# More pairs of an up projection by seven block products, with a worked-out order for the stage

## The chip, the cores and the metric

The kernel runs on one core of a Trainium2 chip. The metric is the device time of one execution in microseconds; the median of three timed runs is given, and one more execution was taken with the hardware profiler.

## What is computed

One transformer block over 512 tokens of width 1024, in fp32. Attention comes first; the change lies in the feed-forward part behind it:

```python
h = rmsnorm(x, mlp_pre_g[i])
gu = h @ w_gate_up[i].astype(h.dtype)          # 1024 -> 2 x 2816
a, u = jnp.split(gu, [D_FF], axis=-1)
a = causal_dwconv(a, conv_w[i], conv_b[i])     # 3 taps along the tokens
y = (jax.nn.gelu(a, approximate=True) * u) @ w_down[i].astype(h.dtype)
x = x + rmsnorm(y, mlp_post_g[i])
```

## The kernel before

Everything is kept transposed: features on the 128 partitions, the 512 tokens along the free axis. Each fp32 operand is split into a high part (ACT rounds it to the float32r type) and a low part (DVE subtracts), and each product is three matmuls: high by high, low by high, high by low (`mm3`).

The hidden width, 2816, makes 22 tiles of 128 rows of `a` and as many of `u`; tile j of both is called pair j here. Pairs 0 to 6 use the input before its normalization (`h2`; the factor `r3` is applied to the results, by POOL too), later ones the normalized input `hn`. A plain pair is two tiles of 8 chunks of 3 matmuls of 512 columns. For the pairs in `BLOCKED`, a 2 x 2 block scheme over (chunk parity) by (token half) needs seven block products in place of eight, each of 4 chunks of 3 matmuls of 256 columns. Its operands are sums: those of the input (`ht`, from `half_sums`) are made once, those of the weights per pair. `gs` holds a pair's four weight blocks. `block_sums_ahead` loads two of them to `y` and two to `x`; POOL then issues three accumulating DMAs, which make y a pair of sums and x two further ones out of y. `blocked_weights` loads the first two blocks once more, for the products that need them plain, and splits all four into high and low parts; each of the six `wh` buffers takes one part of 1024 columns. `blocked_tile` collects the seven products in four PSUM banks and puts them together with one ACT copy and five DVE operations. Then come the convolution (one ACT instruction, two DVE taps), the gelu on ACT, the product with `u` on DVE (mul), and the split of y (`keep_y`: yhi on ACT, ylo on DVE).

The order on each engine is set by a scheduler at compile time, by dependencies and priorities; `keep_in_program_order` pins an instruction behind the one traced before it on its engine. Most of this stage isn't pinned, so the scheduler mixes work of neighbouring pairs and of the down stage that follows. That stage begins with one plain row of tiles (c = 6), in whose shadow DVE makes sums of the stage's results (`sums_of`, from the y's) and the low parts of its weights, then goes on with a plain group of weights and further seven-product groups. PSUM has eight banks, under the tags s (3), mm (2), t (2), o (1). Large SBUF buffers come by tags too: `u` (26), `p` (6), `wr` (2, raw weights), `wh` (6), `kn`, `pt`, `tt`.

Of the kernel before, what the change touches and what calls it, by code (L numbers as in the profile page):

```python
# [81 lines left out]
class Block:  # L82
# [1068 lines left out]
    def conv(self, j, c, a):  # L1151

        nc = self.nc
        w = lambda k: self.col(C_CW + 3 * j + k)
        nc.scalar.activation(c, a, AF.Identity, bias=self.col(C_CB + j), scale=w(2))
        for k in (1, 2):
            nc.vector.scalar_tensor_tensor(c[:, k:], a[:, : T - k], w(2 - k), c[:, k:], op0=ALU.mult, op1=ALU.add)  # L1157
        nc.scalar.activation(c, c, AF.Gelu_apprx_tanh)  # L1158

    def keep_y(self, j, c):  # L1160
        nc = self.nc
        y = self.u([P, 2, T], F32R, YTAG[j])
        nc.scalar.activation(y[:, 0, :], c, AF.Copy)
        nc.vector.tensor_sub(y[:, 1, :], c, y[:, 0, :].bitcast(F32))
        self.y.append(y)

    def mlp_tile(self, j, pa, pu):
        nc = self.nc
        c = self.s([P, T])
        if j <= RAW_LAST:  # L1170
            a = self.s([P, T], tag="as")
            nc.vector.tensor_mul(a, pa, self.r3)
            self.conv(j, c, a)
            nc.gpsimd.tensor_mul(c, c, self.r3)  # L1174
        else:
            self.conv(j, c, pa)
        nc.vector.tensor_mul(c, pu, c)
        self.keep_y(j, c)

    def normalized(self, x1):  # L1180

        nc = self.nc
        fs = []
        for k in range(KC):
            if k % 2 == 0:
                f = self.u([P, 2, T])
                fs.append(f)
            v = f[:, k % 2, :]
            h = self.u([P, 2, T], F32R)
            nc.vector.scalar_tensor_tensor(v, x1[k // 2][:, k % 2, :], self.col(C_GMLP + k), self.r3, op0=ALU.mult, op1=ALU.mult)  # L1190
            nc.scalar.activation(h[:, 0, :], v, AF.Copy)
            nc.vector.tensor_sub(h[:, 1, :], v, h[:, 0, :].bitcast(F32))
            self.hn.append(h)
            yield
        while len(self.y) <= RAW_LAST:
            yield
# [336 lines left out]
```

## Time and profile before

| | |
|---|---|
| median of 3 timed runs | 654.81 us (654.17 to 654.83) |
| the profiled execution's own time | 654.41 us |
| its span, first to last instruction | 652.7 us |
| busy: PE, DVE, ACT, POOL | 645.0, 489.3, 359.7, 174.4 us |
| stretch of pairs 10 to 21 (five plain, seven blocked) | 359.48 to 484.45 us |

The span is what the trace shows; the execution's time has 1.7 us more around it. PE is TensorE's matmuls, DVE VectorE, ACT ScalarE, POOL GpSimd, SP SyncE, which issues most loads. An engine's busy time says nothing alone: PE sets the time where it is never left waiting, another engine where PE waits for it. Durations of single instructions can overlap on one engine, so the distance from start to start is given where it matters. Matmul ends are modelled; starts are what is compared.

### The profile page before, as it was taken

How to read it: one execution, taken by the hardware profiler on the slowest of the kernel's cores; microseconds unless marked ns; L12 is line 12 of the kernel's file. 1: busy time of each engine (PE TensorE's matmuls, PEld its weight loads, DVE VectorE, ACT ScalarE, POOL GpSimd, SP SyncE). 2: the span in 40 equal slices, each digit the busy share in tenths (PEclk: the TensorE clock that was granted, in tenths of full speed). 3: DMA queues.
4: the chain of work that ended last, by engine and by line, in shares of the span. 5: the costliest groups of instructions: out<-in, count | busy, mean ns of one | idle time of the engine just before them, and what ended most of it. 6: DMA issues, size and time to landing. Idle time of an engine off the chain costs nothing.

```text
span 652.7 us, 10523 instructions
## 1 busy us (share of the span) xinstructions
PE 645.0 (99%) x3701; PEld 563.1 (86%) x3701; DVE 489.3 (75%) x1002; ACT 359.7 (55%) x667; POOL 174.4 (27%) x256
## 2 busy tenths in 40 slices
PE   9999999999999999999999999999999999999997
PEld 8988778878888888888888999999988999999986
DVE  6794687978756469689999587777798675756873
ACT  7453687978888476346455354643545433343351
POOL 1111588678486150002131111212000010201000
PEclk9999999999999999999999999999999999999999
DMA  8436721211364528322258879898543434377032
GB/s 305 168 105 198 210 66 32 66 34 51 81 189 166 162 96 290 129 91 71 82 146 209 210 158 266 225 258 219 127 137 109 145 88 121 112 258 259 2 114 80
DMA packets 42484, 95.20 MB, mean 146 GB/s; under 512 B 4416, under 2 KB 13760, under 8 KB 42176
## 3 DMA queue, kind: packets, MB, share of 16 engines
q1 hardware_dynamic: 38112, 85.54, 40.4%
q0 software_dynamic: 4176, 8.91, 8.2%
q8 instruction: 29, 0.48, 0.3%
q14 instruction: 23, 0.19, 0.1%
q10 hardware_dynamic: 144, 0.08, 0.0%
HBM read 77.22 MB, written 9.44 MB: 133 GB/s over the span
## 4 chain that ended last, share of the span: by engine, by line
PE 89%; DVE 4%; ACT 3%; DMA 2%; issue 1%; POOL 1%; ACTq 0%; DVEq 0%
PE mlpup_pss L168 4%; PE mlpup_pss L169 4%; PE mlpup_pss L165 4%; PE mlpup_psmm L165 3%; PE mlpup_psmm L168 3%; PE mlpup_psmm L169 3%; PE nsa_pso L609 2%; PE nsa_pst L576 2%; PE mlpup_pst L168 2%; PE mlpup_pst L165 2%; PE mlpdown_psmm L165 2%; PE mlpup_pst L169 2%; PE mlpdown_psmm L168 2%; PE mlpdown_psmm L169 2%; PE mlpdown_pst L169 2%; PE mlpdown_pst L168 2%
## 5 line engine op out<-in xcount | busy, mean ns | idle before, releaser
L144 ACT ACTIVATE mlpup_wh<-mlpup_wr 128x1024 fp32r<-128x1024 f32 x31 | 32.7, 1055 | 41.6 <-DMA mlpup_wr<-in_gs_dram 20.9
L148 DVE TENSOR_TENSOR mlpup_wh<-mlpup_wr,mlpup_wh 128x1024 fp32r<-128x1024 f32 x31 | 38.6, 1247 | 19.9 <-ACT mlpup_wh L144 15.6
L144 ACT ACTIVATE mlpdown_wh<-mlpdown_wr 128x1024 fp32r<-128x1024 f32 (+1 forms) x27 | 26.6, 987 | 41.1 <-PE mlpdown_pst L168 13.4
L148 DVE TENSOR_TENSOR mlpdown_wh<-mlpdown_wr,mlpdown_wh 128x1024 fp32r<-128x1024 f32 (+1 forms) x27 | 31.1, 1153 | 20.1 <-ACT mlpdown_wh L144 19.9
L599 POOL TENSOR_SCALAR nsa_u<-nsa_u,nsa_nrc,gate 128x512 f32<-128x512 f32 (+3 forms) x64 | 38.7, 620 | 15.1 <-DVE nsa_nrc L735 10.0
L287 POOL TENSOR_TENSOR mlpdown_s<-mlpdown_s,mlpdown_s 128x512 f32<-128x512 f32 x6 | 9.8, 1632 | 118.7 <-ACT mlpdown_s L286 118.6
L701 ACT ACTIVATE nsa_u<-nsa_u,nsa_nnm 128x512 f32<-128x512 f32 (+3 forms) x64 | 35.4, 554 | 7.1 <-DVE nsa_nnm L694 6.9
L168 PE MATMUL mlpup_pss<-mlpup_u,mlpup_wh 128*128 128x512 f32 (+1 forms) x108 | 36.6, 339 | 0.2 <-DVE mlpup_wh L148 0.2
L165 PE MATMUL mlpup_pss<-mlpup_u,mlpup_wh 128*128 128x512 f32 (+1 forms) x108 | 36.5, 338 | 0.0
L169 PE MATMUL mlpup_pss<-mlpup_u,mlpup_wh 128*128 128x512 f32 (+1 forms) x108 | 36.4, 337 | 0.0
L581 DVE TENSOR_TENSOR nsa_u<-nsa_pst,nsa_u 128x512 fp32r<-128x512 f32 (+1 forms) x43 | 29.4, 685 | 6.8 <-ACT nsa_u L578 6.5
L1203 POOL DMA_DIRECT2D mlpup_u<-mlpup_u x14 | 12.4, 885 | 79.1 <-DMA mlpup_u<-mlpup_u 29.0
L1174 POOL TENSOR_TENSOR mlpup_s<-mlpup_s,r3b 128x512 f32<-128x512 f32 x7 | 11.0, 1576 | 77.9 <-ACT mlpup_s L1158 77.9
L148 POOL TENSOR_TENSOR fill_wh<-fill_wr,fill_wh 128x1024 fp32r<-128x1024 f32 (+2 forms) x13 | 24.5, 1888 | 26.5 <-ACT fill_wh L144 26.5
L694 DVE CUSTOM_DVE_ANT_0 nsa_u<-nsa_pss,biastables_u 128x224 f32<-128x224 f32 (+3 forms) x64 | 27.8, 447 | 3.3 <-PE nsa_pss L635 2.7
L578 ACT ACTIVATE nsa_u<-nsa_pst 128x512 fp32r<-128x512 f32 x43 | 25.4, 593 | 8.5 <-PE nsa_pst L576 8.0
L168 PE MATMUL mlpup_psmm<-mlpup_u,mlpup_wh 128*128 128x512 f32 (+1 forms) x88 | 29.9, 340 | 0.0
L169 PE MATMUL mlpup_psmm<-mlpup_u,mlpup_wh 128*128 128x512 f32 (+1 forms) x88 | 29.9, 340 | 0.0
L165 PE MATMUL mlpup_psmm<-mlpup_u,mlpup_wh 128*128 128x512 f32 (+1 forms) x88 | 29.9, 340 | 0.0
L1158 ACT ACTIVATE mlpup_s<-mlpup_s 128x512 f32<-128x512 f32 x22 | 13.9, 631 | 27.2 <-DVE mlpup_s L1157 27.1
L168 PE MATMUL mlpup_pst<-mlpup_u,mlpup_wh 128*128 128x256 f32 (+1 forms) x88 | 26.5, 301 | 0.0
L165 PE MATMUL mlpup_pst<-mlpup_u,mlpup_wh 128*128 128x256 f32 (+1 forms) x88 | 26.5, 301 | 0.0
(548 smaller groups left out, 2367.3 us busy)
## 6 DMA issues: line engine op xcount, KB each, us to landing
mlpup_wr<-in_gu_dram SPq DMA_DIRECT2D x24, 512.0 KB, 3.4
mlpup_u<-in_gs_dram SPq DMA_DIRECT2D x14, 512.0 KB, 5.3
mlpup_u<-in_gs_dram POOLq DMA_DIRECT2D x7, 512.0 KB, 6.3
mlpup_u<-mlpup_u POOLq DMA_DIRECT2D x14, 256.0 KB, 3.6
mlpup_wr<-in_gs_dram SPq DMA_DIRECT2D x7, 512.0 KB, 4.4
mlpdown_wr<-in_down_dram SPq DMA_DIRECT2D x7, 512.0 KB, 3.6
fill_wr<-in_win_dram SPq DMA_DIRECT2D x6, 512.0 KB, 4.0
fill_u<-fill_u SPq DMA_DIRECT2D x20, 128.0 KB, 2.8
```

Of the source, the lines that this page charges most:

```text
L144: h = nc.scalar.activation(hi, raw, AF.Copy)
L148: l = eng.tensor_sub(lw, raw, hi.bitcast(F32))
L165: r = self.pin(mm(ps, hi, x[:, 0, :], start=start, stop=False))
L168: mm(ps, lo, x[:, 0, :], start=False, stop=False)
L169: self.last = mm(ps, hi, x[:, 1, :], start=False, stop=stop).ins
L576: self.att(nc.tensor.transpose(pt[:, r * P : (r + 1) * P], src, self.ident))
L578: nc.scalar.activation(t[:, 0, :], pt, AF.Copy)
L581: nc.vector.tensor_sub(t[rs, part, :], pt[rs], t[rs, 0, :].bitcast(F32))
L599: self.nc.gpsimd.tensor_scalar(ap, ap, col, gate, op0=ALU.mult, op1=ALU.mult)
L694: nc.vector.tensor_tensor_reduce(dst, src, dist, op0=ALU.add, op1=ALU.min, scale=SLOPES[8 + 4 * g + r], scalar=start, accum_out=out)
L701: nc.scalar.activation(dst, dst, AF.Exp, bias=nm[:, r, b : b + 1], scale=-1.0, accum_out=sm[:, r, b : b + 1])
L1158: nc.scalar.activation(c, c, AF.Gelu_apprx_tanh)
```

## The change

All of pairs 10 to 21 are blocked. Per blocked pair, block sums of the weights change hands: y is still made by one accumulating DMA from POOL (y+), while x is loaded once, split as it is (A), then turned in place into the two further sums by two DVE adds (x0, x1) and split again (X). The products go to three banks (f, e, g) instead of four, in the order 1, 2, 5, 6, 4, 3, 7: f's left half takes products 1, 6 and 7 in turn, e's right half 5 and 3, and between them ACT copies what is there so far to SBUF, so that sums accumulate in place. Two DVE operations (q, w) finish them. The plain fourth block D gets its parts in a `u` buffer instead of `wh`.

The whole up stage from pair 2 on is no longer left to the scheduler. Every operation is noted with an engine, a planned duration, what it depends on, a due time and the buffers it takes and frees; `order` plays them as a list schedule (on PE, SP and POOL's DMA queue in the order given, on ACT and DVE the operation that can start first, and of these the one that is due first), and `play` issues them in the resulting order, each ACT, DVE and SP instruction and the first matmul of each product pinned.

```diff
-BLOCKED = [10, 12, 13, 15, 16, 18, 20]
+BLOCKED = [10, 11, 12, 13, 14, 15, 16, 17, 18, 19, 20, 21]
...
+LAG_US = 0.15
+LOAD_US = 6.0
+ISSUE_US = 0.5
+AHEAD_US = 21.0
+PLAIN_US, BLOCK_US = 10.9, 10.1
...
-        x, y = (self.u([P, D], F32, "p") for _ in range(2))
+        y = self.u([P, D], F32, "p")
         self.nc.sync.dma_start(two(y), src(slice(0, 3, 2)))
-        self.nc.sync.dma_start(two(x), src(slice(0, 2)))
         self.pinned = self.last
         self.accumulate(two(y), src(slice(2, 4)))
-        self.accumulate(x[:, :T], y[:, T:])
-        self.accumulate(x[:, T:], x[:, :T])
...
+    def play(self, units):
+
+        for t, _, k in self.order(units):
+            for r in self.ops[k]["run"]() or ():
+                self.held(r)
...
+        us = 1.06 if n == D else .63
...
+        self.op((key, "hi"), "ACT", us, high, deps, due - 1.6, ready, takes=(tag,))
+        self.op((key, "lo"), "DVE", us + .17, low, ((key, "hi"),), due, frees=frees)
...
+    def blocked_ops(self, j, t, cyc):
...
+        step = BLOCK_US / 7
...
+        self.op((j, "y"), "SP", LOAD_US, load_y, ready=t - AHEAD_US, takes=("p",))
+        self.op((j, "y+"), "SWQ", 8.0, second, ((j, "y"),), ready=t - AHEAD_US)
+        xtag = "x" if j < 14 else "p"
+        self.load_op(t - 15, (j, "x"), (D, src(slice(0, 2))), xtag)
+        self.load_op(t - 7, (j, "d"), (T, gs[3]), "wr")
+        xs = lambda: w[j, "x"]
+        self.split_ops((j, "A"), xs, D, t, (((j, "x"), "load"),), ready=t - 8)
+        self.op((j, "x0"), "DVE", .69, lambda: [nc.vector.tensor_add(xs()[:, :T], xs()[:, :T], w[j, "y"][:, T:])],
+                (((j, "A"), "lo"), (j, "y+")), t + .7)
+        self.op((j, "x1"), "DVE", .69, lambda: [nc.vector.tensor_add(xs()[:, T:], xs()[:, T:], xs()[:, :T])],
+                ((j, "x0"),), t + 1.4)
+        self.split_ops((j, "Y"), lambda: w[j, "y"], D, t + 2 * step, ((j, "y+"),), ready=t - 5, frees=("p",))
+        self.split_ops((j, "X"), xs, D, t + 3 * step, ((j, "x1"),), ready=t - 3, frees=(xtag,))
+        self.split_ops((j, "D"), lambda: w[j, "d"], T, t + 4 * step, (((j, "d"), "load"),), "u", ready=t - 1.5, frees=("wr",))
...
+        for name, run, deps, c, due in (
+            ("1", product(("f", a), "A", 0, x(0, a), ends=False), (lo("A"), ("hn", KC - 1, "lo")), copy("q", a, "f", a), 3),
+            ("2", product(("e", a), "A", 4, x(1, a)), (), None, 0),
+            ("5", product(("e", b), "Y", 4, op(0), ends=False), (lo("Y"),) + (("ht", KC // 2 - 1, "lo1"),),
+             copy("w", b, "e", b, -1.0), 5),
+            ("6", product(("f", a), "X", 0, op(1), begins=False, ends=False), (lo("X"), (j, "copy", "1")), copy("q", b, "f", a), 6),
+            ("4", product(("g", a), "D", 0, op(3)), (lo("D"),), copy("w", a, "g", a), 9),
+            ("3", product(("e", b), "X", 4, x(1, b), begins=False), ((j, "copy", "5"),), None, 0),
+            ("7", product(("f", a), "Y", 0, op(2), begins=False), ((j, "copy", "6"),), None, 0),
+        ):
...
+            return [nc.vector.tensor_add(v["q"], v["q"], v["e"])]
...
+            return [nc.vector.tensor_sub(u, u, v["f"][:, None, a].broadcast_to([P, 2, H]))]
...
+        for k in range(KC):
+            t = due + k * PLAIN_US / 16 - 1.6 * (KC - k)
+            self.op(("hn", k), "DVE", .76, functools.partial(value, k), ("r3",) + ((("hn", k - 1, "hi"),) if k else ()), t - 2.4)
...
+        for i in range(4 * DRAM_SUMS):
+            self.op(("copy", i), "SP", 5.0, lambda: next(copies)(), ready=at[DOWN_SUMS] + 10 + i * .5)
+            self.op(("add", i), "SWQ", 5.0, add, (("copy", i),), ready=at[DOWN_SUMS] + 10.2 + 5 * i)
```

The other operations of the stage (normalization, sums of the input, convolution, plain pairs) compute what they did before, now through `op` as well, with planned durations of 0.70 us for a 512-wide DVE operation and 0.76 for a tap.

## Rows read from the trace of the kernel before

**Rows 1.** The page: part 1, busy us of each engine (share of the span, instructions), and of part 2 the granted TensorE clock in 40 equal slices, in tenths of full speed.

```profile
PE 645.0 (99%) x3701; PEld 563.1 (86%) x3701; DVE 489.3 (75%) x1002; ACT 359.7 (55%) x667; POOL 174.4 (27%) x256
...
PEclk9999999999999999999999999999999999999999
```

**Rows 2.** Windows from one pair's first product to the next's, and the whole stretch of pairs 10 to 21: its length, then busy us (instructions) of each engine, granted clock, DMA share, GB/s. 359.48, 380.38, 390.84, 411.75 and 421.74 begin blocked pairs (10, 12, 13, 15, 16), 369.48 a plain one (11).

```profile
369.48:380.38 10.90, 10.90 (x50) 9.01 (x49) 4.64 (x7) 3.53 (x5) 1.77 (x2) 1.00 0.76 191
380.38:390.84 10.46, 10.26 (x85) 10.05 (x84) 8.97 (x12) 5.80 (x9) 1.22 (x1) 1.00 0.70 143
390.84:400.84 10.00, 10.00 (x86) 10.00 (x85) 8.33 (x12) 5.94 (x8) 2.04 (x3) 1.00 1.00 336
...
411.75:421.74 9.99, 9.99 (x85) 9.99 (x84) 7.55 (x12) 4.90 (x7) 2.09 (x2) 1.00 0.90 205
421.74:431.74 10.00, 10.00 (x86) 10.00 (x85) 6.25 (x9) 5.44 (x8) 1.59 (x3) 1.00 0.93 288
...
359.48:484.45 124.97, 124.77 (x829) 115.10 (x828) 93.95 (x133) 59.22 (x81) 19.14 (x20) 1.00 0.79 206
```

**Rows 3.** Timeline of PE inside pair 12: start, duration, instruction, operands, and in brackets the idle time before it and who ended it.

```profile
387.41 0.28 PE L169 MATMUL mlpup_pso<-mlpup_u,mlpup_wh 128*128 128x256 f32 x1
387.53 0.28 PE L165 MATMUL mlpup_pss<-mlpup_u,mlpup_wh 128*128 128x256 f32 x1
388.01 0.39 PE L168 MATMUL mlpup_pss<-mlpup_u,mlpup_wh 128*128 128x256 f32 x1 [0.20 <-DVE mlpup_wh L148]
388.23 0.28 PE L169 MATMUL mlpup_pss<-mlpup_u,mlpup_wh 128*128 128x256 f32 x1
```

**Rows 4.** The chain of waits that led to that instant: start, us, what.

```profile
366.60 8.06 DMA mlpup_wr<-in_gs_dram
...
386.74 1.23 DVE mlpup_wh L148
```

**Rows 5.** DVE's groups of instructions between 340 and 484 us, shapes kept apart: count, then busy us and the mean ns of one, then idle time before them.

```profile
L148 DVE TENSOR_TENSOR mlpup_wh<-mlpup_wr,mlpup_wh 128x1024 fp32r<-128x1024 f32 x19 | 23.2, 1222 | 18.4 <-ACT mlpup_wh L144 14.1 <-issue 2.3 <-ACT mlpup_s L1158 0.9
...
L1157 DVE SCALAR_TENSOR_TENSOR mlpup_s<-mlpup_s,cols,mlpup_s 128x510 f32<-128x510 f32 x7 | 5.2, 747 | 0.1
...
L1245 DVE TENSOR_TENSOR mlpup_wh<-mlpup_wr,mlpup_wh 128x512 fp32r<-128x512 f32 x7 | 4.8, 681 | 0.0
...
L1276 DVE TENSOR_TENSOR mlpup_s<-mlpup_s,mlpup_s 128x512 f32<-128x512 f32 x6 | 4.1, 689 | 3.0 <-ACT mlpup_s L1158 3.0
```

**Rows 6.** Timeline of DVE inside pair 12, and one pair of taps later (x2 merges two instructions): start, duration, instruction.

```profile
387.87 1.22 DVE L148 TENSOR_TENSOR mlpup_wh<-mlpup_wr,mlpup_wh 128x1024 fp32r<-128x1024 f32 x1
389.01 1.22 DVE L148 TENSOR_TENSOR mlpup_wh<-mlpup_u,mlpup_wh 128x1024 fp32r<-128x1024 f32 x1
390.14 0.41 DVE L1269 TENSOR_TENSOR mlpup_s<-mlpup_s,mlpup_pss 128x256 f32<-128x256 f32 x1
390.59 0.42 DVE L1270 TENSOR_TENSOR mlpup_s<-mlpup_s,mlpup_pss 128x256 f32<-128x256 f32 x1
390.93 0.41 DVE L1271 TENSOR_TENSOR mlpup_s<-mlpup_s,mlpup_pso 128x256 f32<-128x256 f32 x1
391.26 0.68 DVE L1274 TENSOR_TENSOR mlpup_s<-mlpup_pso,mlpup_s 128x512 f32<-128x512 f32 x1
391.86 0.67 DVE L1272 TENSOR_TENSOR mlpup_s<-mlpup_s,mlpup_psmm 128x512 f32<-128x512 f32 x1
...
406.15 1.53 DVE L1157 SCALAR_TENSOR_TENSOR mlpup_s<-mlpup_s,cols,mlpup_s 128x511 f32<-128x511 f32 x2
```

**Rows 7.** ACT's groups between 340 and 484 us, columns as in rows 5: a 1024-wide high part, and the copy of half a bank.

```profile
L144 ACT ACTIVATE mlpup_wh<-mlpup_wr 128x1024 fp32r<-128x1024 f32 x19 | 20.1, 1057 | 32.6 <-DMA mlpup_wr<-in_gs_dram 20.9 <-DMA mlpup_wr<-in_gu_dram 6.7 <-PE mlpup_pss L169 3.1
...
L1268 ACT ACTIVATE mlpup_s<-mlpup_pss 128x256 f32<-128x256 f32 x5 | 1.8, 365 | 0.0
```

**Rows 8.** Landing times of the accumulating DMAs that POOL issues (first row, L1203) and of the loads that SP issues ahead of them (second row, L1211), over the whole span.

```profile
DMA to landing us min/median/max: 3.3/6.0/10.7
...
DMA to landing us min/median/max: 3.7/5.3/6.2
```

**Rows 9.** Timeline of DVE and of PE around the end of pair 7's first tile; L1192 writes the last normalized chunk's low part, L169 is the product that reads it, and the L165 at 332.06 is the next tile's first.

```profile
331.92 0.68 DVE L1192 TENSOR_TENSOR mlpup_u<-mlpup_u,mlpup_u 128x512 fp32r<-128x512 f32 x1
...
332.06 0.39 PE L165 MATMUL mlpup_pst<-mlpup_u,mlpup_wh 128*128 128x512 f32 x1
...
333.19 0.61 PE L169 MATMUL mlpup_pst<-mlpup_u,mlpup_wh 128*128 128x512 f32 x2
```

**Rows 10.** The seam to the down stage: busy us (instructions) of each engine in a window for the sums (tile mlpdown_u) and for the weights (mlpdown_wh) alone; the window after the seam, all instructions; then the low part of the first plain group's weights on DVE, and its first product on PE.

```profile
469.00:484.45 15.45, 0.00 (x0) 0.00 (x0) 6.43 (x13) 0.47 (x1) 1.00 0.52 161
...
469.00:484.45 15.45, 0.00 (x0) 0.19 (x1) 2.45 (x2) 2.11 (x2) 1.00 0.52 161
...
484.45:499.30 14.85, 14.85 (x67) 12.25 (x66) 14.85 (x28) 8.04 (x13) 0.00 (x0) 1.00 0.27 86
...
493.54 1.22 DVE L148 TENSOR_TENSOR mlpdown_wh<-mlpdown_wr,mlpdown_wh 128x1024 fp32r<-128x1024 f32 x1
...
499.25 0.39 PE L165 MATMUL mlpdown_pst<-mlpup_u,mlpdown_wh 128*128 128x512 f32 x1
```

**Rows 11.** What DVE waited for between 359 and 485 us: us in total, times, longest.

```profile
DVE mlpup_u L1164 <- ACT mlpup_u L1163: 3.3, 5, 0.7
...
DVE mlpup_s L1276 <- ACT mlpup_s L1158: 3.0, 4, 0.8
```

More of the change, by code (lines that the diff above doesn't have):

```diff
@@ L1149, in pair_of_tiles @@
             self.square_acc(acc, m[:, k, :], False)
[L1151 to L1196, printed above, removed]
-        for kp, f in enumerate(fs):
-            parts = [self.u([P, 2, T], F32R, PTAG[2 * kp + i]) for i in range(2)]
-            self.ht += parts
-            yield from self.half_sums([[f[:, i, hs] for hs in HALF] for i in range(2)], self.u([P, 4, H]), parts)
     def accumulate(self, o, a):
@@ new lines, in load_y, with second @@
+        def load_y():
+            r = w[j, "y"] = self.u([P, D], F32, "p")
+            return [nc.sync.dma_start(two(r), src(slice(0, 3, 2)))]
+        def second():
+            self.pinned = self.last
+            self.accumulate(two(w[j, "y"]), src(slice(2, 4)))
+            self.pinned = None
+        self.op((j, "y"), "SP", LOAD_US, load_y, ready=t - AHEAD_US, takes=("p",))
+        self.op((j, "y+"), "SWQ", 8.0, second, ((j, "y"),), ready=t - AHEAD_US)
+        xtag = "x" if j < 14 else "p"
@@ new lines, in blocked_ops, with summed, rest @@
+        due = t + BLOCK_US + 8
+        def summed():
+            v["c"] = self.s([P, T])
+            return [nc.vector.tensor_add(v["q"], v["q"], v["e"])]
+        def rest():
+            u = two(v["w"])
+            return [nc.vector.tensor_sub(u, u, v["f"][:, None, a].broadcast_to([P, 2, H]))]
+        self.op((j, "q"), "DVE", .7, summed, ((j, "product", "3"), (j, "copy", "6")), due - 6, takes=("s",),
+                frees=("ps" + tags["e"],))
+        self.conv_ops(j, lambda: v["c"], lambda: v["q"], (j, "q"), due - 1, ("s",))
@@ L1312, in mlp_up @@
         cyc = itertools.cycle(["s", "o", "t", "t", "s", "mm", "s", "mm"])
-        pp = {}
-        n = 0
-        self.ahead_sums = {}
-        todo = self.normalized(x1)
-        copies, adds = self.down_copies(), None
+        self.ops, self.w = {}, {}
+        at, t = {}, 0.0
         for j in range(NB // 2, NFF):
-            if j == AHEAD:
-                self.block_sums_ahead(BLOCKED[0])
+            at[j] = t
+            t += BLOCK_US if j in BLOCKED else PLAIN_US
+        for j in range(NB // 2, NFF):
@@ L1345, in mlp_up @@
-            if j >= DOWN_SUMS:
-                for c in copies:
-                    c()
-                adds = adds or self.down_additions()
-                self.pinned = self.last
-                for _ in range(3):
-                    next(adds, lambda: None)()
-                self.pinned = None
-        for a in adds:
-            a()
+                self.blocked_ops(j, at[j], cyc)
+            else:
+                self.plain_ops(j, at[j], self.h2 if j <= RAW_LAST else self.hn, cyc,
+                               ahead[2 * j - NB : 2 * j - NB + 2] if j < NB else None)
@@ new lines, in mlp_up @@
+            if j == NB // 2:
+                ops = self.ops
+                sums = []
+                self.op("sums", "PE", .5, lambda: sums.append(self.row_sums(self.acc3)), (), takes=("pst",))
+                keys = list(ops)
+                first = keys.index((j, "product", 0, KC - 1)) + 1
+                self.ops = {k: ops[k] for k in keys[:first] + ["sums"] + keys[first:-1]}
+                self.root_ops(sums)
+                for k in range(NB // 2):
+                    self.consume_ops(k, pss[2 * k : 2 * k + 2], ("pss", "psmm"), (), (), 21.0 + k)
```

283 lines of the change are left out of this document (223 added, 60 removed).

## The prediction

> **What bounds the kernel now.** I read the page first: PE is busy for 645.0 of 652.7 us and its granted clock never leaves the top step, which is the 2.4 GHz level [rows 1]. So a change pays only if it takes matmul columns away, and only as long as the other engines keep up. DVE, at 75%, is the nearest of them. Next come the windows by pair in the stretch that the change rebuilds [rows 2]: a plain pair lasts 10.90 us, a blocked one 10.00 (5 x 10.90 + 7 x 10.00 and the stall below make up the whole row). In both PE is full. One blocked pair, the first of two blocked in a row, lasts 10.46. The PE timeline there shows why: a matmul starts 0.48 us after the one before it and the next 0.22 later, where 0.12 is the rule, and the wait is for a weight's low part from DVE [rows 3]. The chain of waits leads back from it to a weight load of 8.06 us, with the ACT and DVE work on weights behind it [rows 4]. The whole stretch from pair 10 to pair 21 takes 124.97 us and DVE is busy in 93.95 of it [rows 2], so there is DVE time to spend, about 31 us.
>
> **The change part by part.**
>
> *Five more blocked pairs (11, 14, 17, 19, 21).* With seven products instead of eight, all twelve pairs last 12 x 10.00 = 120.0 us if nothing stalls, against 124.97 now. That is 4.97 us: 5 x 0.90 for the products and 0.46 for the stall of [rows 3], which also goes if the seams are clean. Matmul shapes and counts of a blocked pair stay (7 x 12 of 256 columns), so 10.00 holds.
>
> *DVE per blocked pair.* Removed: three half-width and two full adds (L1269 to L1274). Added: the two weight sums x0 and x1 (512 wide), q and w. Left: four low parts, two taps, mul, ylo. Durations are 1.22 us for a 1024-wide low part, 0.68 to 0.69 for a 512-wide two-input operation and 0.75 for a tap [rows 5]. But starts are closer than durations: 1.13 to 1.14 after a 1024-wide one, 0.60 after a 512-wide one, and 0.11 more where an operation reads what the one before it wrote (0.45 against 0.34 at half width; two taps in a row take 1.53, so start 0.78 apart) [rows 6]. An independent tap I put at 0.66, its duration less the 0.09 that the others overlap by. Summed by starts: 3 x 1.14 for A, Y, X; 0.60 for D; 0.60 and 0.71 for x0 and x1; 0.60 q; 0.66 and 0.78 for the taps; 0.60 w; 0.71 mul; 0.60 ylo: 9.28 us in a pair of 10.00. The slack is 0.72 us a pair. Summed by durations it is 3 x 1.22 + 7 x 0.685 + 2 x 0.75 = 9.96, and 10.4 with the 0.03 to 0.04 us that separate dependent operations put behind each of twelve. I take 9.28, because the run of seven operations in [rows 6] is this very mix and keeps to the starts; both ends stay for the range.
>
> The Trainium skill speaks against this choice: VectorE: DVE Perf Modes, section "The DRAIN you can't avoid", says that the next operation does not start until the pipe has emptied, and the errata section gives (N + 151) / 0.96 ns for an fp32 two-input operation, 1224 ns at 1024 columns and 691 at 512. The durations of [rows 5] agree with it, the starts of [rows 6] do not. By the page, as an estimate from its formula, the DVE sum would be 3 x 1.22 + 9 x 0.69 = 9.9 us a pair with no gap left, which is what the first rival below works out from the rows.
>
> *ACT copies.* Four of 0.37 us a pair [rows 7] in place of one. ACT is busy for 4.9 to 5.9 us of a blocked pair's window now [rows 2], so for at most 7.0 then. Each in-place bank has two products, 2 x 1.43 = 2.86 us, between the product that fills it and the next that adds to it. The copy needs 0.37 plus at most one 1.06 us conversion in front of it, 1.43 us. Hidden; if ACT's queue is held by a wait for over 1.4 us, PE stops for the rest. Cost 0, bound 0 to the 0.46 of a seam, below.
>
> *Transfers.* A blocked pair loses the separate 512 KB load of x, now shared with A, and two 256 KB on-chip accumulations. That leaves three SP loads and one accumulation on POOL, in place of four and three; POOL has nothing else in these pairs. The one that matters is y+, since x0, then X's low part, then the product that adds to f wait for it. Landing takes at most 10.7 us and the load before it at most 6.2 [rows 8]: 16.9 of the 21 us by which y is ordered ahead. Cost 0. Behind a late y+ on POOL stand only the next pair's y+ and the four down-stage additions.
>
> *The order, pinned.* Every ACT, DVE and SP operation of the stage now stands where the planner put it, so a wait holds all that is behind it. The planner reckons 1.23, 0.70 and 0.76 us for what starts every 1.14, 0.60 and 0.66, and 0.15 for a hand-over. With fixed orders, an engine whose operations are all shorter than planned gets to none of them later than planned. Its DVE sum a pair is 10.19 against 10.1 of PE: full, but the chip has 9% in hand. For the eleven seams between blocked pairs, the bounds are 0 (the seam of the pairs at 411.75 and 421.74 has none) and 11 x 0.46 = 5.1 (each like the other seam) [rows 2]. I take 0.3: the 8.06 us load that made that stall is now ordered 15 us ahead, but the wh slots of X come free only as the pair before ends.
>
> *Pair 7.* Its last normalized chunk is written at 331.92 to 332.60, and its first tile hid that by letting that tile's last product slip to 333.4, past the next tile's first [rows 9]. Pinned products can't slip: up to 0.54 us (332.60 less 332.06). But these chunks now have due times ahead of the tails of earlier pairs. I take 0.2.
>
> *The seam to the down stage.* DVE already works for it: 6.43 us on sums and 2.45 on weights lie between 469 and 484.45 [rows 10], because pair 21 was plain. A blocked pair 21 needs 4.4 us more DVE time (9.28 less 2 x 1.14 + 0.66 + 0.78 + 2 x 0.60), so about half of that work moves behind the seam. What is late next is the weights of the first plain group: their low part ends at 494.76, PE wants it at 499.25 [rows 10], so 4.5 us are covered. Bounds: 0, and 8.9 - 4.5 = 4.4 if nothing is done ahead. In the last pair no next pair's weights are prepared (A, x0, x1, 2.4 us), so I take 0.5.
>
> **Sum.** -4.97 + 0.3 + 0.2 + 0.5 = -3.97. The profiled execution took 654.41 us (span 652.7 and 1.7 around it), so 650.4. The median of the timed runs is 654.81, 0.4 above it: 650.8 there.
>
> **Rivals.**
>
> 1. *DVE becomes the bound.* If twelve dense pairs run by durations, 10.4 us a pair, PE waits 12 x 0.4 = 4.8 us, and with the 0.7 of the last two terms the time is 654.9, or 655.3 timed: no change. For: the durations, and the same DVE load in every pair where plain ones used to give relief. Against: [rows 6], and the 14.85 us from 484.45 on, which DVE fills from end to end while PE does too [rows 10].
> 2. *Every seam stalls like the one in [rows 3].* 5.1 instead of 0.3: 655.2, or 655.6 timed: no change. For: X's slots. Against: the other seam. By measurement, 1.3 us (0.2%) is what can be told from no change.
> 3. *Slower: the pinned DVE queue stands still at ACT's round trips.* Today DVE waits 0.75 us for the gelu before a blocked pair's mul and 0.66 before ylo [rows 11]. If the pinned order has nothing to put there, it loses 1.41 us a pair: 9.28 + 1.41 = 10.69, and 12 x 0.69 = 8.3 us of PE waiting give 658.4, or 658.8 timed. It decides from 0.72 us of forced idle a pair on; beyond 1.1 it eats the whole gain. For: two such trips in each of twelve pairs, and no later operation may step in. Against: the planner models both engines and puts the next pair's low parts in between.
>
> That the change doesn't do what it says can be left out for the products, which are fixed in the code.
>
> **Chances.** The forecast, with its own range from 649.6 to 652.5 timed: 0.66. The forecast with most of the down-stage debt or several seams, 652.5 to 653.5: 0.05. Rival 1: 0.09, rival 2: 0.08, rival 3: 0.12. So faster 0.71, same 0.17, slower 0.12. The range goes from 649.3 (no stall at all, 649.8, less the spread of the runs) to 655.4, into rival 1 and part of rival 2, and leaves out a fifth.
>
> **What would show it.** Right: windows of 10.0 us for each pair from 10 to 21, the down stage starting about 4.5 us earlier than 484.45, DVE busy for 9.3 to 9.6 us of each, no PE wait for a low part. Wrong: PE waits for L148-like low parts with DVE full in the window (rival 1), with DVE idle for ACT (rival 3), or at the third and fourth product of each pair alone (rival 2); a gap at the first plain group of the down stage says that the debt was mis-sized; a gap before pair 7's second tile says the same of the start.

## The result, and the profile after

The changed kernel takes 651.32 us (median; 650.73 to 651.72), the kernel before 654.77 beside it on the same chip: a ratio of 0.995, 95% interval 0.9937 to 0.9963. That is faster by 0.5%, 3.45 us, where 4.0 was forecast (650.8). The profiled execution took 650.98 us, 3.43 less than that of before; its span is 649.3 us.

The page of the changed kernel, the rows that answer [rows 1]:

```profile
PE 641.5 (99%) x3881; PEld 568.9 (88%) x3881; DVE 510.2 (79%) x1025; ACT 382.2 (59%) x718; POOL 170.6 (26%) x247
...
PEclk9999999999999999999999999999999999999999
```

TensorE stays the bound at its full clock, with 3.5 us less work; VectorE has 21 us more. The windows, which answer [rows 2]: pairs 10, 11, 19 and 20, pair 21 up to its last product in two parts, and the whole from pair 10 to 479.83.

```profile
360.05:370.09 10.04, 10.04 (x86) 10.04 (x84) 7.91 (x11) 5.60 (x10) 1.22 (x1) 1.00 0.67 183
370.09:380.13 10.04, 10.04 (x87) 10.04 (x85) 9.27 (x13) 6.92 (x12) 1.19 (x1) 1.00 0.59 135
...
450.41:460.45 10.04, 10.04 (x87) 10.04 (x85) 9.21 (x13) 6.46 (x11) 2.93 (x3) 1.00 0.86 267
460.45:471.00 10.55, 10.30 (x87) 10.10 (x86) 9.37 (x13) 7.47 (x13) 0.00 (x0) 1.00 0.94 236
471.00:479.83 8.83, 8.83 (x76) 8.78 (x74) 8.83 (x14) 3.18 (x5) 1.57 (x2) 1.00 0.60 122
479.83:485.30 5.47, 5.47 (x27) 4.51 (x25) 5.47 (x11) 2.63 (x5) 0.00 (x0) 1.00 0.42 120
360.05:479.83 119.78, 119.53 (x999) 119.28 (x997) 108.73 (x144) 77.31 (x124) 14.13 (x13) 1.00 0.65 170
```

Every pair is a blocked one of 10.04 us, and only pair 20 is longer, 10.55. VectorE is busy in about 9.2 us of each but the first, in 108.73 of these 119.78 where it was 93.95 over 124.97. Pair 21 is mixed with the first matmuls of the down stage; no step in it is longer than usual, so it is taken at 10.04 too. With that the change in the stage's length can be read off: 12 x 10.04 + 0.51 = 120.99 against 124.97, 3.98 less.

Two places gave something back. TensorE's timeline at pair 20 and at pair 7 (start, duration, instruction, idle time before it and who ended it), which answers [rows 3] and [rows 9]:

```profile
464.76 0.28 PE L169 MATMUL mlpup_pss<-mlpup_u,mlpup_wh 128*128 128x256 f32 x1
465.28 0.38 PE L172 MATMUL mlpup_pss<-mlpup_u,mlpup_wh 128*128 128x256 f32 x1 [0.25 <-DVE mlpup_wh L1255]
465.50 0.28 PE L173 MATMUL mlpup_pss<-mlpup_u,mlpup_wh 128*128 128x256 f32 x1
...
327.04 0.39 PE L169 MATMUL mlpup_pst<-mlpup_u,mlpup_wh 128*128 128x512 f32 x1
327.50 0.50 PE L172 MATMUL mlpup_pst<-mlpup_u,mlpup_wh 128*128 128x512 f32 x1
327.84 0.39 PE L173 MATMUL mlpup_pst<-mlpup_u,mlpup_wh 128*128 128x512 f32 x1
```

At pair 20 two steps take 0.52 and 0.22 us where 0.12 is the rule: 0.51 lost. At pair 7 the step from 327.04 takes 0.46 where 0.23 is the rule, and with 0.11 in the next one 0.35 is lost; before, there was no stall there. So the up stage is 3.98 - 0.35 = 3.63 us shorter. The span is 3.4 shorter, since this execution reached the up stage 0.2 us later, behind work that the change leaves alone.

The chain of waits behind pair 20's stall, TensorE's own rows left out (start, us, what), answers [rows 4]:

```profile
451.81 0.57 SPq L295
...
453.69 0.70 SPq L295
454.43 7.23 DMA mlpup_wr<-in_gs_dram
...
463.02 0.96 ACT mlpup_wh L1252
464.00 1.24 DVE mlpup_wh L1255
```

Four copies for the down stage (L295) stand in SyncE's queue ahead of the load of pair 20's D. The load starts 2.6 us later than it could and takes 7.23 us to land; ScalarE, in its fixed order, waits for it, and X's high and low part, which stand behind, come late.

### The profile page after: what moved, and what is told of

Its sections match the earlier page's. It is cut to its first block, busy times and chain, and to the rows that moved or that the text cites. A ratio compares the mean times of both kernels' runs of the same rounds, so it can differ in the third digit from the quotient of the medians.

```text
span 649.3 us, 10899 instructions
## 1 busy us (share of the span) xinstructions
PE 641.5 (99%) x3881; PEld 568.9 (88%) x3881; DVE 510.2 (79%) x1025; ACT 382.2 (59%) x718; POOL 170.6 (26%) x247
## 4 chain that ended last, share of the span: by engine, by line
PE 86%; DVE 7%; ACT 3%; POOL 2%; DMA 1%; issue 1%; SPq 0%; ACTq 0%; DVEq 0%
PE mlpup_pss L172 3%; PE mlpup_pss L173 3%; PE mlpup_pss L169 3%; PE mlpup_pst L172 2%; PE nsa_pso L613 2%; PE nsa_pst L580 2%; PE mlpdown_psmm L169 2%; PE mlpdown_psmm L172 2%; PE mlpdown_psmm L173 2%; PE mlpup_pst L169 2%; PE mlpup_pst L173 2%; PE mlpdown_pst L169 2%; PE mlpdown_pst L172 2%; PE mlpdown_pst L173 2%; PE mlpup_psmm L169 2%; PE mlpup_psmm L173 2%
## 5 line engine op out<-in xcount | busy, mean ns | idle before, releaser
L1252 ACT ACTIVATE mlpup_wh<-mlpup_u 128x1024 fp32r<-128x1024 f32 x41 | 43.1, 1054 | 13.9 <-PE mlpup_pss L172 4.8
L1255 DVE TENSOR_TENSOR mlpup_wh<-mlpup_u,mlpup_wh 128x1024 fp32r<-128x1024 f32 x41 | 49.7, 1217 | 1.0 <-ACT mlpup_wh L1252 1.0
L152 DVE TENSOR_TENSOR mlpdown_wh<-mlpdown_wr,mlpdown_wh 128x1024 fp32r<-128x1024 f32 (+1 forms) x27 | 31.3, 1161 | 17.4 <-ACT mlpdown_wh L148 14.6
L1159 POOL DMA_DIRECT2D mlpup_u<-in_gs_dram x12 | 14.7, 1225 | 110.0 <-DVE mlpup_wh L1255 72.6
L172 PE MATMUL mlpup_pss<-mlpup_u,mlpup_wh 128*128 128x256 f32 (+1 forms) x124 | 36.8, 297 | 0.2 <-DVE mlpup_wh L1255 0.2
L169 PE MATMUL mlpup_pss<-mlpup_u,mlpup_wh 128*128 128x256 f32 (+1 forms) x124 | 36.8, 296 | 0.0
L173 PE MATMUL mlpup_pss<-mlpup_u,mlpup_wh 128*128 128x256 f32 (+1 forms) x124 | 36.7, 296 | 0.0
L1303 POOL TENSOR_TENSOR mlpup_s<-mlpup_s,r3b 128x512 f32<-128x512 f32 x7 | 13.8, 1984 | 73.1 <-ACT mlpup_s L1280 73.1
L152 POOL TENSOR_TENSOR fill_wh<-fill_wr,fill_wh 128x1024 fp32r<-128x1024 f32 (+2 forms) x13 | 24.6, 1893 | 26.5 <-ACT fill_wh L148 26.5
L1278 DVE SCALAR_TENSOR_TENSOR mlpup_s<-mlpup_s,cols,mlpup_s 128x511 f32<-128x511 f32 (+1 forms) x38 | 29.6, 782 | 0.2
L172 PE MATMUL mlpup_pst<-mlpup_u,mlpup_wh 128*128 128x256 f32 (+1 forms) x88 | 26.7, 303 | 0.1
L169 PE MATMUL mlpup_pst<-mlpup_u,mlpup_wh 128*128 128x256 f32 (+1 forms) x88 | 26.6, 302 | 0.0
L173 PE MATMUL mlpup_pst<-mlpup_u,mlpup_wh 128*128 128x256 f32 (+1 forms) x88 | 26.6, 302 | 0.0
L613 PE MATMUL nsa_pso<-nsa_u,vnatural_u 128*128 128x512 f32 x72 | 25.8, 424 | 0.4 <-DVE nsa_s L597 0.2
L169 PE MATMUL mlpdown_psmm<-mlpup_u,mlpdown_wh 128*128 128x512 f32 (+1 forms) x76 | 26.2, 345 | 0.0
```

The costliest lines, as they stand in the source:

```text
L152: l = eng.tensor_sub(lw, raw, hi.bitcast(F32))
L169: r = self.pin(mm(ps, hi, x[:, 0, :], start=start, stop=False))
L172: mm(ps, lo, x[:, 0, :], start=False, stop=False)
L173: self.last = mm(ps, hi, x[:, 1, :], start=False, stop=stop).ins
L613: self.att(nc.tensor.matmul(po, v, t[:, part, :], start=start, stop=stop))
L1252: return [nc.scalar.activation(w[key][0], src(), AF.Copy)]
```

## The experiments

Times are medians; the ratio is to the kernel before on the same chip. The second row is the yardstick for those that come near the changed kernel:

> The changed kernel itself once more, unaltered, as the yardstick for the two runs beside it and for the earlier ones: 650.7 to 651.7 us, a ratio of 0.995 to the kernel before.

| what runs | us | ratio, 95% interval |
|---|---|---|
| the changed kernel | 651.32 | 0.9950 (0.9937 to 0.9963) |
| the same again | 650.73 | 0.9955 (0.9943 to 0.9968) |
| old seven pairs | 654.19 | 1.0003 (0.9994 to 1.0012) |
| one VectorE addition more a pair | 654.47 | 1.0003 (0.9990 to 1.0016) |
| three more a pair | 671.37 | 1.0266 (1.0244 to 1.0287) |
| no pins | 654.22 | 1.0000 (0.9990 to 1.0009) |
| down copies later | 652.42 | 0.9970 (0.9959 to 0.9982) |
| pair 7's weights earlier | 651.04 | 0.9949 (0.9935 to 0.9962) |
| both | 651.68 | 0.9965 (0.9952 to 0.9978) |
| both, and blocked from pair 9 | 654.47 | 1.0004 (0.9996 to 1.0013) |
| r3 multiplied on VectorE | 655.35 | 1.0026 (1.0015 to 1.0037) |
| pins up to pair 9 alone | 650.64 | 0.9952 (0.9938 to 0.9965) |
| that, and pair 7's weights earlier | 649.78 | 0.9932 (0.9919 to 0.9945) |

**Where the gain lies: the old seven pairs in the new scheme.**

```diff
-BLOCKED = [10, 11, 12, 13, 14, 15, 16, 17, 18, 19, 20, 21]
+BLOCKED = [10, 12, 13, 15, 16, 18, 20]
```

> The changed kernel (651.3 us) with the list of blocked pairs put back to the old seven (10, 12, 13, 15, 16, 18, 20); the products in place, the weight sums on VectorE and the pinned order of the up stage stay. Theory: the gain is that of the five pairs 11, 14, 17, 19 and 21 alone, each 0.86 us shorter blocked (10.90 plain against 10.04 in the changed kernel's windows), so 4.3 us of it go: about 654.5 to 655.6, no faster than the kernel before. Rival: the new scheme and the pinned order gain by themselves, by taking stalls away; then the time stays well below 654, at 651 to 653.

It took 654.19 us, 0.3 under the theory's range and no faster than the kernel before. Its windows of pairs 12 and 13, and of pairs 10 to 21:

```profile
381.11:391.13 10.02, 10.02 (x86) 10.01 (x84) 7.27 (x10) 6.03 (x10) 0.00 (x0) 1.00 0.41 98
391.13:401.15 10.02, 10.02 (x87) 10.02 (x86) 7.80 (x11) 6.49 (x11) 1.22 (x1) 1.00 0.86 287
360.19:485.00 124.81, 124.81 (x830) 115.30 (x829) 96.50 (x127) 67.26 (x101) 10.52 (x10) 1.00 0.60 168
```

The stretch lasts 124.81 us where it was 124.97. The seam behind pair 12 is clean, so the 0.46 of [rows 3] did not belong to seams as such; whether the old load alone made it, this run doesn't separate. Some 0.3 of it is lost again in pairs that are each 0.02 to 0.03 us longer. Pair 7's stall of 0.35 is here too. So the new scheme and the worked-out order bring nothing by themselves; the gain is that of the five pairs. No run blocks all twelve pairs in the old scheme, so whether the five could have been had without the in-place sums isn't shown.

**How near VectorE is: additions put into each blocked pair.** The loop has one round, or three.

```diff
+        for i in range(1):
+            self.op((j, "more", i), "DVE", .7, lambda: [nc.vector.tensor_add(self.more, self.r3, self.r3)],
+                    ((j, "product", "1"),), t + (i + 2) * step)
...
+        self.more = self.rp.tile([P, T], F32, tag="rb", name="more")
```

> The changed kernel with one added VectorE addition of 512 columns (float32, into a tile that nothing reads) in each of the twelve blocked pairs, spread by the planner like the taps. Theory: VectorE is busy 9.2 us of a blocked pair's 10.04 in the changed kernel, and one more operation of 0.60 us from start to start makes about 9.8, which still fits: the time rises by at most 1 us, to 651.3 to 652.3. Rival: the durations of the records add up on VectorE (9.96 us a pair by the sum of the prediction, and 0.66 to 0.75 for the added one): 10.65 against 10.04, some 0.6 us in each of twelve pairs, 7 us, 658.

> The same with three added VectorE additions in each blocked pair. Theory of the starts: 9.2 and 3 x 0.60 make 11.0 us a pair where TensorE wants 10.04, so VectorE becomes the bound and twelve pairs take 0.96 us more each: 11.5 us, about 663. Theory of the durations: 9.96 and 3 x 0.68 make 12.0, 1.96 more in each pair, 23 us, about 675. If VectorE is not near its limit at all, the time stays at 651 to 653.

With one, the time rose to 654.47 (652.65 to 655.97, the widest spread of all runs), the whole gain and over three times what the theory allowed. The windows of one of the longer pairs and of nine pairs on end:

```profile
409.75:420.08 10.33, 10.30 (x86) 10.10 (x85) 10.04 (x14) 6.85 (x12) 1.22 (x1) 1.00 0.71 184
...
379.63:471.15 91.52, 91.40 (x758) 90.59 (x757) 87.18 (x115) 59.58 (x97) 10.13 (x9) 1.00 0.65 176
```

A pair now takes 91.52 / 9 = 10.17 us, with stalls of 0.29 in four of the nine, none of them in the first three; the larger loss comes at the end, where pair 21's last weights and the first down tile's come late (what TensorE waited for between 256 and 520 us: total, times, longest):

```profile
PE mlpdown_psmm L172 <- DVE mlpdown_wh L152: 1.6, 1, 1.6
PE mlpup_pso L172 <- DVE mlpup_wh L1255: 1.0, 1, 1.0
```

With three it took 671.37. Eight pairs on end, and VectorE's timeline around two of the additions:

```profile
379.73:470.26 90.53, 84.47 (x674) 81.23 (x673) 88.89 (x121) 52.55 (x87) 10.13 (x9) 1.00 0.56 150
```

```profile
403.60 1.22 DVE L1255 TENSOR_TENSOR mlpup_wh<-mlpup_u,mlpup_wh 128x1024 fp32r<-128x1024 f32 x1
404.74 1.41 DVE L1425 TENSOR_TENSOR more<-r3b 128x512 f32<-128x512 f32 x2
406.06 1.22 DVE L1255 TENSOR_TENSOR mlpup_wh<-mlpup_u,mlpup_wh 128x1024 fp32r<-128x1024 f32 x1
```

VectorE is busy for 88.89 of 90.53 us and sets a pair's length, 90.53 / 8 = 11.32. Two additions take 1.32 us from start to start, one alone 0.60, so three come to 1.8 to 2.0, and 9.3 to 9.5 are left for the pair itself. That is the forecast's 9.28 by starts, not the 9.96 by durations: the arithmetic holds. What fell is the step from slack to safety. On paper one addition still fits (9.4 + 0.6 = 10.0 of 10.04); on the chip the pair became 0.13 longer and more was lost at the seam to the down stage. That a debt of all twelve pairs comes due there is a reading of these waits; no run separates it from what the seam would lose anyway. The changed kernel stands one 512-wide operation a pair from losing its gain. (The time itself lies between the 663 and the 675 of the two theories. Of the 20 us that three cost, eight pairs of 1.28 more make 10.2. Pair 20 alone took 16.23, with a stop of 3.32 us for a high part from ScalarE and a granted clock of 0.89, and what follows it lost 3.9; neither theory foresaw these.)

The runs also bear on the rule that was weighed. The section "The DRAIN you can't avoid" of VectorE: DVE Perf Modes (the Trainium skill) has the next operation start only when the pipe is empty, and adds that one which is not held starts earlier. By its first half alone a pair with three more additions would take, as an estimate from the durations, 9.96 + 3 x 0.68 = 12.0 us; the 11.32 decides against that here, and starts that come 0.08 to 0.09 us before the end of the operation in front fit the second half.

**What the pins are for: off from the first blocked pair on, and all off.**

```diff
-                self.held(r)
+                if t < self.pins_end:
+                    self.held(r)
...
+        self.pins_end = at[BLOCKED[0]]
```

The run without any pins (both edits free SyncE's loads of the stage too, since these go through the same helper):

```diff
     def held(self, r):
-        return self.tc.keep_in_program_order(r)
+        return r
```

> The changed kernel with its twelve blocked pairs, but the operations of the up stage on VectorE, ScalarE and GpSimd are not kept in the order that the planner worked out: the scheduler orders them by its own estimates, as in the kernel before (TensorE's own order stays). Theory A: at 9.2 of 10.04 us a pair VectorE has so little room that the order decides; without it products wait, by 0.5 us in many of the twelve pairs, 654 to 658. Theory B: the fifth part of work that VectorE has spare is enough under either order, and the time stays within 0.5 us of the changed kernel, 650.8 to 651.8.

> The changed kernel with the order pinned only for what the planner starts before the first blocked pair; the blocked pairs' operations on VectorE, ScalarE and GpSimd are left to the scheduler. Theory: the pins are worth their 3.3 us (the kernel without any pins against the changed kernel) in the stretch of r's third sum and pairs 5 to 9 alone; the kernel without pins had no stall in its blocked pairs, not even the one at pair 20. So here too they run without a stall: 650.5 to 651.3. Rival: part of the pins' worth lies in the blocked pairs, or in how what comes early stands against the loads of the blocked pairs: 652 or more.

Without any pins the time was 654.22, within theory A's range, but not by its mechanism. TensorE's only wait, and two windows (the granted clock stands behind the five engines):

```profile
299.64 0.39 PE L173 MATMUL mlpup_pss<-r_u,mlpup_wh 128*128 128x512 f32 x1
302.54 0.47 PE L169 MATMUL mlpup_psmm<-r_u,mlpup_wh 128*128 128x512 f32 x1 [2.51 <-DVE mlpup_s L1309]
```

```profile
302.54:307.20 4.66, 4.66 (x14) 3.67 (x15) 4.66 (x6) 2.47 (x4) 1.30 (x1) 0.63 0.04 15
...
364.11:474.40 110.29, 110.29 (x925) 110.29 (x924) 101.16 (x129) 73.80 (x119) 12.24 (x12) 1.00 0.68 177
```

In the plain pairs behind r3 the multiplication that frees a bank (L1309) comes late. VectorE's rows ahead of it:

```profile
297.20 1.78 DVE L1278 SCALAR_TENSOR_TENSOR mlpup_s<-mlpup_s,cols,mlpup_s 128x510 f32<-128x510 f32 x1
...
300.04 1.75 DVE L1278 SCALAR_TENSOR_TENSOR mlpup_s<-mlpup_s,cols,mlpup_s 128x511 f32<-128x511 f32 x1
301.71 0.68 DVE L1309 TENSOR_TENSOR mlpup_s<-mlpup_psmm,mlpup_s 128x512 f32<-128x512 f32 x1
```

The scheduler's order has a low part and a tap in front of it, and two taps there last 1.78 and 1.75 us, where 0.74 is usual, while GpSimd multiplies (from 296.97 and from 299.85). So the order and this slowing make the delay together; their shares aren't separated. TensorE stops for 2.5 us, and for the 4.66 us behind it the granted clock is 0.63 on average: matmuls come every 0.43 us, the 1.2 GHz level, where 0.23 is the rule, and another 1.7 us are lost. The eleven blocked pairs from 364.11 on take 110.29, 10.03 each, without a stall: there, unpinned order is as good. The other run says it directly. With pins up to pair 9 alone it took 650.64, as its theory said, and SyncE's issues show why pair 20 doesn't stall in it:

```profile
449.51 0.34 SPq L1267 DMA_DIRECT2D mlpup_wr<-in_gs_dram  x1
...
451.93 2.46 SPq L295 DMA_DIRECT2D downblocks<-in_gd_dram  x4
```

The load of D (L1267 here) is no longer pinned; it is issued at 449.51, ahead of the copies, and lands in 3.0 us. So the pins are worth some 3 us in the plain pairs behind r3 and nothing in the blocked ones.

**The two stalls.** The copies 4 us later, then pair 7's weights planned 3 us earlier, then both:

```diff
-            self.op(("copy", i), "SP", 5.0, lambda: next(copies)(), ready=at[DOWN_SUMS] + 10 + i * .5)
-            self.op(("add", i), "SWQ", 5.0, add, (("copy", i),), ready=at[DOWN_SUMS] + 10.2 + 5 * i)
+            self.op(("copy", i), "SP", 5.0, lambda: next(copies)(), ready=at[DOWN_SUMS] + 14 + i * .5)
+            self.op(("add", i), "SWQ", 5.0, add, (("copy", i),), ready=at[DOWN_SUMS] + 14.2 + 5 * i)
```

```diff
-                self.split_ops((j, i), lambda i=i: w[j, i, "raw"], D, s, (((j, i, "raw"), "load"),), frees=(tag,))
+                self.split_ops((j, i), lambda i=i: w[j, i, "raw"], D, s - 3 * (j == RAW_LAST + 1), (((j, i, "raw"), "load"),), frees=(tag,))
```

> The changed kernel with the four copies of the down weights on SyncE's queue (and the additions into them on GpSimd's queue) given ready times 4 us later, so that the load of pair 20's D stands ahead of them in the queue. Theory: the stall of 0.5 us at pair 20 comes from that load being issued 2.6 us late behind the copies; it goes, and the time falls by 0.5 us to about 650.8. Rival: the stall has another cause (ScalarE's own order, or the transfer's own time of 7.2 us), and it stays: 651.3; or the copies, now later, make the down stage's first tiles late, and the 0.5 us come back there.

> The changed kernel with the splitting of pair 7's weights planned 3 us earlier. Theory: the stall of 0.35 us more than before at pair 7's second product is a weight's low part that VectorE finishes late; planned earlier it is there in time and 0.35 us go, 651.0. Rival: VectorE is full since the third sum of r and each operation moved ahead pushes another one back by as much: the stall moves to another product, and the time stays at 651.3.

> Both edits, the later copies and the earlier splitting of pair 7's weights. If both theories hold, 0.5 and 0.35 add up to 0.85 us: about 650.5. If the planner's order changes as a whole with either edit, the sum is less.

The later copies took pair 20's stall away, as the theory said, and the time was 652.42 all the same. Only part of that is in the trace: in three of the six executions 2.4 to 3.4 us lie outside the span, where 1.7 is usual. What they are stays open. By the medians of the spans, 649.85 against 649.0 for the second row on the same chip, 0.85 us are lost. VectorE's timeline in the run with both edits, then in the changed kernel:

```profile
503.75 0.69 DVE L1598 COPY mlpdown_u<-mlpdown_psmm 128x512 f32<-128x512 f32 x1 [2.40 <-PE mlpdown_psmm L173]
504.36 0.95 DVE L152 TENSOR_TENSOR mlpdown_wh<-mlpdown_u,mlpdown_wh 128x768 fp32r<-128x768 f32 x1
```

```profile
502.19 0.95 DVE L152 TENSOR_TENSOR mlpdown_wh<-mlpdown_u,mlpdown_wh 128x768 fp32r<-128x768 f32 x1
504.55 0.69 DVE L1598 COPY mlpdown_u<-mlpdown_psmm 128x512 f32<-128x512 f32 x1 [1.41 <-PE mlpdown_psmm L173]
```

In the down stage, whose order the scheduler makes, the copy that empties the first tile's bank (L1598) has come to stand ahead of the next weights' low part (L152). VectorE waits 2.40 us for that tile while the low part stands behind, and TensorE waits 1.2 us for it. The run with the later copies alone has the same two instructions turned round and the same wait of 1.2 us, so a shift of 4 us in the up stage's copies did it, 50 us later. The run with both edits took 651.68 where 650.5 was expected.

In the run with the earlier weights both stalls are gone: 360.65 to 481.13 us is 12 x 10.04, and no wait of the up stage is left. Pair 7's went by the edit. Pair 20's went by chance: the copies still stand ahead of D's load, and the order on every engine round it is the changed kernel's. ScalarE's high part of D there, first in the changed kernel, then in this run:

```profile
461.68 0.63 ACT L1252 ACTIVATE mlpup_u<-mlpup_wr 128x512 fp32r<-128x512 f32 x1 [1.53 <-DMA mlpup_wr<-in_gs_dram]
```

```profile
461.76 0.63 ACT L1252 ACTIVATE mlpup_u<-mlpup_wr 128x512 fp32r<-128x512 f32 x1 [1.01 <-DMA mlpup_wr<-in_gs_dram]
```

The load took 7.2 us to land in the changed kernel and 0.51 was lost, 7.0 in its other profile and 0.22 was lost, 6.8 here and nothing was. Where D's load stands ahead of the copies (the runs with later copies and with pins up to pair 9), no wait is left there. So its place in the queue puts the load at the edge, and its landing time then decides whether TensorE waits. Yet 651.04 can't be told from the changed kernel. The profiled executions reach the up stage's first product at anything from 249.6 to 251.2 us, by code that no edit touches (250.25 in the changed kernel, 251.22 in this run): a gain of 0.5 to 0.9 us is at the edge of what medians of this kernel tell.

**One pair more, and the multiplication by r3.**

```diff
-BLOCKED = [10, 11, 12, 13, 14, 15, 16, 17, 18, 19, 20, 21]
+BLOCKED = [9, 10, 11, 12, 13, 14, 15, 16, 17, 18, 19, 20, 21]
```

> Both edits, and pair 9 is blocked too, thirteen pairs in all. Theory: 0.86 us less for one more pair where VectorE keeps up, about 649.6. Rival: VectorE stands behind since pair 7 and has still to make the parts of r that the first blocked pair needs, as much earlier by one pair: the sums of the first blocked pair come late, and the stall costs as much as the pair gains or more, 650.5 to 653.

```diff
-            self.op((j, "r"), "POOL", 1.6, lambda: [nc.gpsimd.tensor_mul(c[0], c[0], self.r3)], ((j, "gelu"),), due - .8)
+            self.op((j, "r"), "DVE", .7, lambda: [nc.vector.tensor_mul(c[0], c[0], self.r3)], ((j, "gelu"),), due - .8)
```

> The changed kernel with the seven multiplications by r3 of pairs 0 to 6 moved from GpSimd to VectorE. Theory: between r3 and pair 8 VectorE and GpSimd slow each other (GpSimd's multiplication takes 1.30 us where it runs beside weight sums and 3.34 at the worst, VectorE's two-input operations 1.68 to 1.79 beside it where 0.60 to 0.66 is usual), and VectorE once waits 1.18 us for GpSimd. Seven more operations cost VectorE 7 x 0.60 = 4.2 us; three slowed operations, another 0.3 us longer, and the wait give back some 4.6 in the stretch 297 to 322. So VectorE is no fuller than before, pair 7's stall of 0.35 us becomes smaller or goes, and the time is 650.8 to 651.3. Rival: the slowing costs VectorE less than it seems, seven more operations fill it further, and the stall at pairs 7 to 9 grows by up to 4 us: 652 to 655.

Both edits with pair 9 blocked cost all that was gained, 654.47: the rival, and more than it reckoned. VectorE in the windows ahead of the two stalls, and the stalls themselves:

```profile
328.00:343.84 15.84, 15.84 (x71) 13.12 (x70) 15.70 (x27) 9.64 (x14) 4.01 (x3) 1.00 0.90 258
343.84:354.10 10.26, 8.61 (x49) 7.29 (x48) 10.16 (x17) 7.07 (x11) 1.21 (x1) 1.00 0.78 190
```

```profile
345.88 0.50 PE L172 MATMUL mlpup_psmm<-mlpup_u,mlpup_wh 128*128 128x512 f32 x1 [1.65 <-DVE mlpup_wh L1255]
...
355.40 0.39 PE L172 MATMUL mlpup_psmm<-mlpup_u,mlpup_wh 128*128 128x256 f32 x1 [1.02 <-DVE mlpup_wh L1255]
```

VectorE is busy for 25.86 of 26.10 us there (15.70 + 10.16): it has no room for the parts that a blocked pair 9 needs. Two more waits, 1.5 us in all, follow at the down stage's first tile.

The multiplications on VectorE gave 655.35: the time came out just over the rival's 655, while the claim on the engines holds in the main. The stretch from the up stage's start to the same tap, the changed kernel first:

```profile
249.94:328.63 78.69, 78.61 (x346) 64.50 (x345) 69.57 (x88) 41.36 (x59) 11.77 (x6) 1.00 0.34 124
```

```profile
249.63:328.22 78.59, 76.54 (x337) 62.83 (x336) 70.76 (x95) 42.28 (x60) 0.00 (x0) 1.00 0.34 124
```

VectorE reached the same point after 78.59 us instead of 78.69 with six multiplications and one other operation more (95 against 88), which raised its busy time by 1.2 us where 0.60 each would make 4.2. But the order changed with them. One low part, in the changed kernel and in this run:

```profile
291.74 1.22 DVE L1255 TENSOR_TENSOR mlpup_wh<-mlpup_u,mlpup_wh 128x1024 fp32r<-128x1024 f32 x1
```

```profile
300.68 1.22 DVE L1255 TENSOR_TENSOR mlpup_wh<-mlpup_u,mlpup_wh 128x1024 fp32r<-128x1024 f32 x1
```

In the changed kernel it stands where VectorE has to wait for GpSimd anyway; here the planner, which goes by due times, has three of the multiplications and eleven other operations ahead of it, and TensorE stops for 2.05 us at 299.51. Pair 21's last weights and the turned copy of above cost another 2.5 at the end.

**Both stalls taken away together.** The pins up to pair 9 alone, and pair 7's weights 3 us earlier; the edits are those above.

> The changed kernel with the order pinned only up to the first blocked pair (which took the stall at pair 20 away) and pair 7's weights planned 3 us earlier (which took the stall at pair 7 away). Theory: both stalls are gone, 0.35 and 0.2 to 0.5 us less than the changed kernel, a ratio of 0.994 to 0.995 to the kernel before, about 650.2. Rival: with the weights earlier another wait takes its place, as the 0.19 us before the down stage's last statistics in the run with the earlier weights, and nothing is left to measure: 650.6 to 651.2.

649.78 us, the fastest of all and 0.4 under the theory's 650.2; it is 4.4 under the kernel before on the same chip where the changed kernel is 3.0 to 3.5 under. No wait of TensorE is left in the up and down stages. The intervals of the two still overlap (0.9919 to 0.9945 and 0.9937 to 0.9963), so the firmer evidence is the trace, in which both stalls are gone.

## Why the prediction was right, point by point

- **The five pairs, -4.97.** Right in kind and nearly in size: 12 x 10.04 against 124.97 is -4.49. A blocked pair is 10.04 and not 10.00; 12 x 0.04 is the difference. The spacing of matmuls within a product, 118 to 120 ns, differs from product to product and repeats in every pair; with the old seven pairs in the same scheme it gave 10.02, without pins 10.03. What it hangs on stays open.
- **VectorE, 9.28 by starts.** 9.2 by the windows, 9.3 to 9.5 where it is the bound. Rival 1, the durations, is refuted by both. Rival 3, idle time at ACT's round trips, too: VectorE's wait for ScalarE's high part of y (L1291) came to 3.1 us in four of nine pairs from 370 to 460, where 3.3 in five was the sum before [rows 11]. But the margin was read too kindly, as the run with one addition shows. What the prediction set against its own choice, from "The DRAIN you can't avoid" of VectorE: DVE Perf Modes (the Trainium skill), was only the first half of what that section says.
- **The seams, 0.3.** One stall of 0.51 (0.22 in the other profile of the same kernel). The size was near and the cause was not the one named: no slot of `wh`, but D's load behind the down copies. The step that failed is the one on transfers, "cost 0": it followed y+ alone, looked at landing times, and left out that SyncE issues four copies in 2.6 us ahead of a load that is ordered only 7 us before its pair. Rival 2 is refuted: ten of eleven seams are clean.
- **Pair 7, 0.2.** 0.35, and again by another cause. The last normalized chunk was on time; the low part of its first weight was not, because VectorE has been nearly full since r3 (37.5 of the 40 us from 290 on), and its two waits on the way, 1.20 and 1.18 us, are for multiplications on GpSimd (the last section shows the second). Planning the weight earlier removed the stall.
- **The seam to the down stage, 0.5.** 0. VectorE is full there as foreseen (8.83 of 8.83 and 5.47 of 5.47 us), but TensorE had 24 matmuls of the first down tile to do at 479.83, before pair 21's last product at 485.30. This cover was used for pair 7 in the prediction and overlooked here: the pinned products can't slip, but others can slip in front of them. It isn't large: one addition more a pair, and TensorE waits 1.0 and 1.6 us there.
- **ACT, 0.** At most 7.0 us a pair was forecast; 5.60 to 6.92 in the windows above, and 7.47 in pair 20 with its late load. No product waited for a copy in place.

Three terms too small (0.48 for the products, 0.21 and 0.15 for the stalls at pairs 20 and 7) and one too large (0.5) lie between the forecast -3.97 and the -3.63 measured in the up stage. The main term was right by its mechanism. That the rest came out so near is luck: the errors partly cancel, both stalls had other causes than those named, and that at pair 20 varies from one profile to the next.

## What to carry to other kernels

Read an engine's share by the distance of starts, but don't count the rest as room: with VectorE busy for 92% of each pair nothing was lost, at 95% four of nine pairs stalled and more was lost where the next stage begins. When operations move earlier or later, follow every queue that they share: a load that is late by four issues in front of it, or a copy that waits ahead of a weight, can cost more than the operations themselves. In this kernel an order was worth pinning where a run without pins showed a loss, and nowhere else.
